# The first pass multiplies 33 of 44 up-projection weight blocks unsplit in fp32; the second pass splits and writes them

## The chip, the cores and the metric

The kernel runs on one core of a Trainium2 chip. The metric is the device time of one execution in microseconds (us), and lower is better. A change of about 0.3% (some 10 us here) is the least that a measurement of this kernel can tell from no change.

## The reference, cut to what matters

One layer of a hybrid decoder is computed for 2048 prompt tokens and 64 sample tokens, which share every weight. The part that the change touches is the gated feed-forward block:

```
x = x + W_down( SiLU(gate) * val ),  [gate|val] = causal depthwise conv (3) of RMSNorm(x) @ w_up
```

`w_up` is 1024 x 5632 in fp32, 44 blocks of 128 columns (22 for the gate, 22 for the value); `w_down` is 2816 x 1024, 22 blocks here. Around it stand the input projection, a conformer convolution with 31 taps, a gated delta-rule scan, the output projection and a per-layer embedding gate.

## The kernel before, in words

**Passes.** The tokens are worked off in six passes of 256, 384, 384, 384, 384 and 320 columns (`NTS`, the last with the sample tokens). Activations lie transposed in SBUF, channels on the partitions and tokens along the free axis, so a weight block of 1024 x 128 is eight 128 x 128 stationary tiles. The chain of stages of a pass is: input projection, scan and convolution (`units_b`), output projection (`units_w`), norm (`units_norm`), feed-forward (`units_f`), gate (`units_l`). While pass i is in its feed-forward, `merge` strews the scan and the 31-tap convolution of pass i+1 between its units; in the first pass that stretch also inverts the triangular blocks of the second pass (`inv_step`).

**Split products.** Every large product is made of three matmuls in fp32r: each operand x is held as a high part (a rounded copy, `act` at L108 on ScalarE) and a low part (the difference, `tt` at L105 on GpSimd or VectorE; both in `split`, L230). `gemm` (L280) issues for each of the eight k-tiles high x high, high x low and low x high: 24 matmuls for a block.

**Weights.** `get` (L260) keeps three blocks under way and hands out the oldest; `wblock` (L242) loads one. The pool tag "w" has three slots of 1 MB (high and low part). A block that has never been written is loaded raw (512 KB, L248) into one of three slots of the tag "xio", split into the w slot, and the pair of halves is written to DRAM (1 MB, L254). Every later pass loads the halves straight into the w slot (L245). All these DMAs are issued by one queue, SP's, in order. An exception is the set `seen`: 22 of the 44 up blocks and 11 of the 22 down blocks are split in the first pass without being written; the second pass loads them raw once more, splits them and writes them. So the first pass splits 66 blocks of the feed-forward and writes 33; the second splits and writes 33.

**Around it.** `half` (L1211) is one up block: `gemm_w` into a PSUM bank, a copy `row` and a scaled copy `y` on ScalarE, two convolution taps on VectorE (`stt`, L96). `down` (L1245) multiplies `fbuf` by a down block and adds the result to `X` on VectorE. The norm of the residual stream writes each channel block into a small tile `h` (two slots) and splits it into `q.hT2`, which `half` multiplies. The tag "X" has two slots of 128 x 8 x 384 fp32; the residual stream of each pass takes one (L1166, loaded at L1167). Instructions are issued in order on each engine; the order was set when the program was built, by priorities.

**Names in the profile.** L89 is every matmul, L93 every transpose, L96 the scalar_tensor_tensor helper, L105 the tensor_tensor helper, L108 the activation helper. `cacc` is the accumulator of the 31-tap convolution, `hT` stands for `hT2` too, `w<-raw` on POOL is the low part of a split weight block; `d`, `g` and `m` are PSUM banks.

Of the kernel before, what the change touches and what calls it, by code (L numbers as in the profile page):

```python
# [8 lines left out]
F32 = mybir.dt.float32  # L9
# [7 lines left out]
P = 128  # L17
D = 1024
KD = D // P
# [23 lines left out]
def step_kernel(  # L43
# [8 lines left out]
    V, A, G, T, SY = nc.vector, nc.scalar, nc.gpsimd, nc.tensor, nc.sync  # L52

    cpool = ctx.enter_context(tc.tile_pool(name="cpool", bufs=1))
    big = ctx.enter_context(tc.tile_pool(name="big", bufs=1))
    wp = ctx.enter_context(tc.tile_pool(name="wp", bufs=2))
# [10 lines left out]
    def nm(s):  # L67
        uid[0] += 1
        return f"{s}_{uid[0]}"
# [18 lines left out]
    def mm(out, lhsT, rhs, start, stop, skip=True):  # L88
        T.matmul(out, lhsT=lhsT, rhs=rhs, start=start, stop=stop, skip_group_check=skip)  # L89
# [8 lines left out]
    def ts(e, out, in0, s1, op0, s2=None, op1=None):  # L98
        if op1 is None:
            e.tensor_scalar(out=out, in0=in0, scalar1=s1, scalar2=None, op0=op0)  # L100
        else:
            e.tensor_scalar(out=out, in0=in0, scalar1=s1, scalar2=s2, op0=op0, op1=op1)
# [38 lines left out]
    def raw_tile(name, shape=(P, KD, P)):  # L141
        return wp.tile(list(shape), F32, tag="xio", name=nm(name), bufs=3)
# [10 lines left out]
    def h_tile(name="h"):  # L153
        return rp.tile([P, 512], F32, tag="h", name=nm(name), bufs=2)
# [75 lines left out]
    def split(src, hi, lo, hi_e="a", lo_e="g"):  # L230
        if hi_e == "a":
            act(hi, src)
        else:
            V.tensor_copy(hi, src)
        tt(G if lo_e == "g" else V, lo, src, hi.bitcast(F32), SUB)

    halves, seen = {}, set()

    def w_tile():
        return wp.tile([P, 2, KD, P], F32R, tag="w", name=nm("w"), bufs=3)  # L240

    def wblock(key, src, hi_e="a", lo_e="g", nk=KD):  # L242
        w = w_tile()
        if key in halves:
            SY.dma_start(w.bitcast(F32), halves[key])  # L245
        else:
            raw = raw_tile("raw")
            SY.dma_start(raw if nk == KD else raw.rearrange("p (k o) c -> p k (o c)", k=nk), src)  # L248
            split(raw, w[:, 0], w[:, 1], hi_e, lo_e)
            if key[0] in ("w_up", "down") and key not in seen and (key[1] // P + key[-1]) % 2:  # L250
                seen.add(key)
                return w[:, 0], w[:, 1]
            halves[key] = hw.tile([P, 2, KD, P], F32, tag=nm("halves"), name=nm("halves"))
            SY.dma_start(halves[key], w.bitcast(F32))  # L254
        return w[:, 0], w[:, 1]
# [24 lines left out]
    def gemm(ps, w, m, nk):  # L280
        whi, wlo = w
        mhi, mlo = m
        for k in range(nk):
            mm(ps, whi(k), mhi(k), k == 0, False, skip=False)
            mm(ps, whi(k), mlo(k), False, False, skip=False)
            mm(ps, wlo(k), mhi(k), False, k == nk - 1, skip=False)

    def halfs(a):
        return a[:, 0], a[:, 1]

    def gemm_w(ps, w, hT, c0, cw):
        gemm(ps, (lambda k: w[0][:, k, :], lambda k: w[1][:, k, :]),
             (lambda k: hT[0][:, k, c0:c0 + cw], lambda k: hT[1][:, k, c0:c0 + cw]), KD)
# [25 lines left out]
    def token_rs(acc, q):  # L319
        ps = bank()  # L320
        for i, (t, c0, L) in enumerate(q.tiles):
            mm(ps[:L, t:t + 1], acc[:, c0:c0 + L], one1[:, 0:1], i == 0, i == len(q.tiles) - 1)
        v = dp.tile([P, 8], F32, tag="var", name=nm("var"), bufs=2)
        rs = dp.tile([P, 8], F32, tag="rsv", name=nm("rsv"), bufs=2)
        V.memset(v, 1.0)
        ts(V, v[:, 0:q.nt], ps[:, 0:q.nt], 1.0 / D, MUL, EPS, ADD)
        if q.sam:
            ts(V, v[:NSAM, q.nt:q.nt + 1], ps[:NSAM, q.nt:q.nt + 1], 1.0 / D, MUL, EPS, ADD)
        n = len(q.tiles)
        rsqrt(rs[:, 0:n], v[:, 0:n])  # L330
        return rs
# [845 lines left out]
    def units_norm(q):  # L1177
        n = q.n

        def stats():  # L1180
            q.hT2 = big.tile([P, 2, KD, NMAX], F32R, tag="hT2", name=nm("hT2"))
            rs = token_rs(q.acc, q)
            q.dgs = []
            for t, c0, L in q.tiles:
                q.dgs.append(dp.tile([P, P], F32, tag="Zt", name=nm("dg"), bufs=ZB))
                ts(V, q.dgs[-1][:L, :L], ident[:L, :L], rs[:L, t:t + 1], MUL)

        def spread_rs():
            q.nps = ps = bank()
            for i, (t, c0, L) in enumerate(q.tiles):  # L1190
                mm(ps[:, c0:c0 + L], one1[:L, :], q.dgs[i][:L, :L], i == 0, i == len(q.tiles) - 1)

        def part(b):
            h = h_tile()
            stt(V, h[:, :n], q.X[:, b, 0:n], gains[:, b, 1:2], q.nps[:, :n], MUL, MUL)
            split(h[:, :n], q.hT2[:, 0, b, 0:n], q.hT2[:, 1, b, 0:n], "a", "v" if b % 2 else "g")
        return [((), stats), ((), spread_rs)] + [((), lambda b=b: part(b)) for b in range(KD)]


    def units_f(q):  # L1200
        n, np_, sam = q.n, q.np, q.sam
        out = []
        z = {}

        def begin():
            z["f"] = big.tile([P, 2 * FG * 2 * NMAX], F32R, tag="F", name=nm("fbuf"))
            if sam:
                z["st"] = big.tile([P, 2 * FT, 2 * NSQ], F32, tag="zs", name=nm("fst"))
                load_T("fst", [st_ffn[0].rearrange("s r c -> (s r) c")], 2 * DFF, z["st"])

        def half(col):  # L1211
            ffS = W["ff"]
            w = get()
            y = r_tile("y")
            row = r_tile("row", NMAX + 3)
            srow = srow_tile() if sam else None
            G.tensor_copy(row[:, 0:2], ffh[:, col, 0:2])  # L1217
            if sam:
                G.tensor_copy(srow[:, :, 0:2], z["st"][:, col, :].rearrange("p (s r) -> p s r", r=2))
            ps = gbank()  # L1220
            gemm_w(ps[:, :n], w, halfs(q.hT2), 0, n)
            to_row(q, row, srow, 2, ps, lambda o, i, *a: act(o, i))
            act(y[:, :n], ps[:, :n], AF.Identity, scale=ffS[:, col, 2:3], bias=ffS[:, col, 3:4])
            G.tensor_copy(ffh[:, col, 0:2], row[:, np_:np_ + 2])  # L1224
            if sam:
                G.tensor_copy(ffh[:, col, 2:18].rearrange("p (s r) -> p s r", r=2), srow[:, :, 8:10])
            for tap in (1, 0):
                for o, i in taps(q, y, row, srow, tap):
                    stt(V, o, i, ffS[:, col, tap:tap + 1], o, MUL, ADD)
            return y  # L1230

        def ff_ap(slot, hl, j, a, b):
            base = ((slot * FG + j) * 2 + hl) * NMAX
            return z["f"][:, base + a:base + b]

        def gate(f):
            z["g"] = y = half(f)
            act(y[:, :n], y[:, :n], AF.Silu)

        def val(f, slot, j):  # L1240
            y = half(FT + f)
            tt(V, y[:, :n], y[:, :n], z["g"][:, :n], MUL)
            split(y[:, :n], ff_ap(slot, 0, j, 0, n), ff_ap(slot, 1, j, 0, n))

        def down(nk, slot, i):  # L1245
            w = get()
            m = KD // nk
            for o in range(m):
                ps = bank() if q.ip == 0 and o % 2 else gbank()
                gemm(ps[:, :n], (lambda k: w[0][:, k * m + o, :], lambda k: w[1][:, k * m + o, :]),  # L1250
                     (lambda k: ff_ap(slot, 0, k, 0, n), lambda k: ff_ap(slot, 1, k, 0, n)), nk)
                xs = q.X[:, i * m + o, 0:n]
                tt(V, xs, xs, ps[:, :n], ADD)

        out.append(((), begin))
        pend = []
        for g0 in range(0, FT, FG):
            slot = (g0 // FG) % 2
            nk = min(FG, FT - g0)
            for j in range(nk):  # L1260
                f = g0 + j
                out.append(((("w_up", f * P),), lambda f=f: gate(f)))
                out.append(((("w_up", (FT + f) * P),), lambda f=f, slot=slot, j=j: val(f, slot, j)))
            out += pend
            pend = [((("down", g0, i),), lambda nk=nk, slot=slot, i=i: down(nk, slot, i)) for i in range(nk)]
        return out + pend
# [133 lines left out]
    for ip, q in enumerate(ps_):  # L1400
        prev = ps_[ip - 1] if ip else None
        nxt = None if q.sam else ps_[ip + 1]
        w = units_w(q)
        if prev is not None:
            x2 = units_x2(prev)
            w = [u for i in range(KD) for u in (w[i], x2[i])] + x2[KD:]
# [5 lines left out]
        else:  # L1412
            own = [u[1:] for u in u1 if 100 <= u[0] < 100.14 and not u[1]]
            k = len(own) // 2
# [43 lines left out]
```

## Time and profile before

| | us |
|---|---|
| median of 3 runs | 3202.05 (3193.27 to 3202.27) |
| the profiled execution, device time | 3196.92 |
| its span (first to last instruction) | 3195.2 |
| PE busy | 2973.2 |
| DVE busy | 2213.8 |
| ACT busy | 1122.4 |
| POOL busy | 894.5 |

The busy shares are means over stretches with different limits, so they are read stretch by stretch. The feed-forward of the first pass lies between 337 and 690 us of the span, that of the second between about 830 and 1340 us. "PEclk" is the granted clock of TensorE as a share of 2.4 GHz.

### The profile page before, as it was taken

The numbers are of one execution on the slowest core, as the hardware profiler recorded it, in microseconds if no ns is written. First come the engines' busy times: TensorE is split into PE (matmuls) and PEld (weight loads), VectorE is DVE, ScalarE is ACT, GpSimd is POOL, SyncE is SP. The second block draws the span as 40 slices with busy tenths as digits, with TensorE's granted clock in tenths as the row PEclk, the third lists the DMA queues.
The fourth block names the chain that finished last, engine by engine and source line by source line (L and its number), as shares of the span: only waits on it lengthen the run. The fifth ranks groups of instructions, "written<-read, shape, count | busy, mean of one in ns | idle before, by whom it ended". The sixth has DMA issues, their size and how long they took to land.

```text
span 3195.2 us, 51070 instructions
## 1 busy us (share of the span) xinstructions
PE 2973.2 (93%) x18682; PEld 2900.9 (91%) x18682; DVE 2213.8 (69%) x5378; ACT 1122.4 (35%) x2473; POOL 894.5 (28%) x1518
## 2 busy tenths in 40 slices
PE   5979688777999999999999999999999999998998
PEld 5979678677999998999999999999999999998998
DVE  6986889957669686756757666857577866743443
ACT  4333344334323334422234342223442232323223
POOL 3422576634333432211121121121131121111221
PEclk8989898888999999999999999999999999998999
DMA  7636766667777867667665677665767765666885
GB/s 231 203 118 225 239 194 214 185 214 250 297 251 248 271 231 259 237 240 249 228 220 214 237 253 245 228 239 198 249 242 255 261 241 198 219 222 226 301 293 207
DMA packets 291968, 745.28 MB, mean 233 GB/s; under 512 B 51241, under 2 KB 202282, under 8 KB 216575
## 3 DMA queue, kind: packets, MB, share of 16 engines
q1 hardware_dynamic: 291719, 742.03, 67.9%
q8 instruction: 148, 2.42, 0.3%
q14 instruction: 101, 0.83, 0.1%
HBM read 607.75 MB, written 134.57 MB: 232 GB/s over the span
## 4 chain that ended last, share of the span: by engine, by line
PE 64%; DVE 7%; DMA 3%; ACT 1%; issue 1%; SPq 0%; ACTq 0%; DVEq 0%
PE g L89 57%; PE d L89 3%; PE m L89 2%; DMA w<-halves 2%; DVE h L96 1%; PE d L93 1%; PE m L93 1%; DVE y L96 1%; DVE rt L105 1%; DVE hT L105 0%; DMA out_dram<-yt 0%; DVE cacc L96 0%; DVE sy L96 0%; DVE X L100 0%; DVE X L105 0%
## 5 line engine op out<-in xcount | busy, mean ns | idle before, releaser
L89 PE MATMUL g<-hT,w 128*128 128x384 f32 (+2 forms) x9840 | 1684.6, 329 | 38.7 <-ACT hT L108 9.3
L89 PEld LDWEIGHTS g<-hT,w 128*128 128x128 f32 x9840 | 1600.7, 192 | 49.9 <-ACT hT L108 11.0
L89 PE MATMUL g<-fbuf,w 128*128 128x384 f32 (+2 forms) x2904 | 549.4, 338 | 32.8 <-DVE X L105 15.2
L96 DVE SCALAR_TENSOR_TENSOR y<-row,ffS,y 128x384 f32<-128x384 f32 (+1 forms) x528 | 337.6, 639 | 301.8 <-ACT y L108 275.8
L89 PEld LDWEIGHTS g<-fbuf,w 128*128 128x128 f32 x2904 | 489.7, 194 | 43.3 <-DVE X L105 16.8
L96 DVE SCALAR_TENSOR_TENSOR cacc<-H,cfS,cacc 128x384 f32<-128x384 f32 (+1 forms) x696 | 487.4, 700 | 9.3 <-ACT cacc L108 3.0
L105 DVE TENSOR_TENSOR X<-X,g 128x384 f32<-128x384 f32 (+2 forms) x532 | 276.7, 524 | 228.1 <-PE g L89 225.9
L108 ACT ACTIVATE row<-g 128x384 f32<-128x384 f32 (+1 forms) x336 | 152.4, 454 | 598.5 <-PE g L89 594.2
L105 POOL TENSOR_TENSOR w<-raw,w 128x1024 fp32r<-128x1024 f32 x123 | 307.6, 2502 | 193.4 <-ACT w L108 169.9
L1224 POOL COPY ffh<-row 128x2 f32<-128x2 f32 x264 | 61.9, 235 | 594.4 <-ACT row L108 589.5
L89 PE MATMUL g<-x,w 128*128 128x384 f32 (+2 forms) x1152 | 204.1, 331 | 5.9 <-ACT w L108 4.6
L89 PE MATMUL g<-mx,w 128*128 128x384 f32 (+2 forms) x1152 | 193.9, 327 | 12.3 <-DMA w<-halves 9.5
L89 PEld LDWEIGHTS g<-mx,w 128*128 128x128 f32 x1152 | 186.7, 191 | 15.1 <-issue 4.7
L1217 POOL COPY row<-ffh 128x2 f32<-128x2 f32 x264 | 82.8, 314 | 418.2 <-DVE y L96 312.8
L89 PEld LDWEIGHTS g<-x,w 128*128 128x128 f32 x1152 | 192.1, 195 | 6.7 <-ACT w L108 5.0
L108 ACT ACTIVATE y<-g,ffS 128x384 f32<-128x384 f32 (+2 forms) x264 | 169.3, 641 | 0.1
L108 ACT ACTIVATE w<-raw 128x1024 fp32r<-128x1024 f32 x139 | 146.5, 1055 | 63.3 <-PE g L89 14.9
L105 POOL TENSOR_TENSOR fbuf<-y,fbuf 128x384 fp32r<-128x384 f32 (+2 forms) x132 | 136.4, 1034 | 115.0 <-ACT fbuf L108 111.5
L108 ACT ACTIVATE y<-y 128x384 f32<-128x384 f32 (+2 forms) x132 | 65.7, 498 | 217.7 <-DVE y L96 217.4
L108 ACT ACTIVATE fbuf<-y 128x384 fp32r<-128x384 f32 (+2 forms) x132 | 65.8, 498 | 213.5 <-DVE y L105 213.3
L96 DVE SCALAR_TENSOR_TENSOR H<-row,dnS,H 128x384 f32<-128x384 f32 (+1 forms) x144 | 92.8, 646 | 34.2 <-ACT H L108 33.2
L105 POOL TENSOR_TENSOR y<-row,y 128x256 fp32r<-128x256 f32 x48 | 36.2, 754 | 272.7 <-PE m L89 218.1
(338 smaller groups left out, 3291.1 us busy)
## 6 DMA issues: line engine op xcount, KB each, us to landing
w<-halves SPq DMA_DIRECT2D x477, 1024.0 KB
halves<-w SPq DMA_DIRECT2D x106, 1024.0 KB
raw<-in_w_up_dram SPq DMA_DIRECT2D x66, 512.0 KB
raw<-in_w_down_dram SPq DMA_DIRECT2D x33, 512.0 KB
raw<-in_w_in_dram SPq DMA_DIRECT2D x24, 512.0 KB
xt<-in_x_prompt_dram SPq DMA_DIRECT2D x16, 512.0 KB
xT<-xt SPq DMA_DIRECT2D x16, 512.0 KB
out_dram<-yt SPq DMA_DIRECT2D x16, 512.0 KB
```

Source lines behind the costliest of these rows:

```text
L89: T.matmul(out, lhsT=lhsT, rhs=rhs, start=start, stop=stop, skip_group_check=skip)
L93: T.transpose(out, in_, ident[:k, :k])
L96: return e.scalar_tensor_tensor(out=out, in0=in0, scalar=scalar, in1=in1, op0=op0, op1=op1)
L105: e.tensor_tensor(out=out, in0=a, in1=b, op=op)
L108: A.activation(out, in_, f, **kw)
L1217: G.tensor_copy(row[:, 0:2], ffh[:, col, 0:2])
L1224: G.tensor_copy(ffh[:, col, 0:2], row[:, np_:np_ + 2])
```

## The change

For an up block whose column number is not a multiple of 4 (33 of 44), the first pass loads the raw block straight into a w slot as fp32 and returns it as it is; nothing is split or written. `up_gemm` multiplies such a block by the unsplit normed activations with eight fp32 matmuls in place of 24 in fp32r. For that the first pass keeps the normed activations in fp32 (`q.hf`), in a slot of the tag "X" rather than in the small tile `h`. In the second pass these 33 blocks are loaded raw, split and written. The old exception is gone: the 11 other up blocks and all 22 down blocks are split and written in the first pass. The first pass therefore splits 33 blocks and writes 33; the second splits and writes 33, as before, but all of them up blocks.

```diff
     def wblock(key, src, hi_e="a", lo_e="g", nk=KD):
+        if key[0] == "w_up" and key[1] // P % 4 and key not in seen:
+            seen.add(key)
+            w = wp.tile([P, KD, P], F32, tag="w", name=nm("w"), bufs=3)
+            SY.dma_start(w, src)
+            return w
         w = w_tile()
...
             split(raw, w[:, 0], w[:, 1], hi_e, lo_e)
-            if key[0] in ("w_up", "down") and key not in seen and (key[1] // P + key[-1]) % 2:
-                seen.add(key)
-                return w[:, 0], w[:, 1]
             halves[key] = hw.tile([P, 2, KD, P], F32, tag=nm("halves"), name=nm("halves"))
             SY.dma_start(halves[key], w.bitcast(F32))
...
         def part(b):
-            h = h_tile()
+            if q.ip == 0:
+                if b == 0:
+                    q.hf = big.tile([P, KD, n], F32, tag="X", name=nm("hf"), bufs=2)
+                h = q.hf[:, b]
+            else:
+                h = h_tile()
...
+        def up_gemm(ps, w):
+            if isinstance(w, tuple):
+                return gemm_w(ps, w, halfs(q.hT2), 0, n)
+            for k in range(KD):
+                mm(ps, w[:, k, :], q.hf[:, k, :], k == 0, k == KD - 1, skip=False)
...
             ps = gbank()
-            gemm_w(ps[:, :n], w, halfs(q.hT2), 0, n)
+            up_gemm(ps[:, :n], w)
```

## Rows read from the trace of the kernel before

**Rows 1.** The page: busy time in all, and tenths in 40 slices of 80 us.
```profile
PE 2973.2 (93%) x18682; PEld 2900.9 (91%) x18682; DVE 2213.8 (69%) x5378; ACT 1122.4 (35%) x2473; POOL 894.5 (28%) x1518
...
DVE  6986889957669686756757666857577866743443
...
POOL 3422576634333432211121121121131121111221
```
**Rows 2.** Windows: stretch, length, busy us of each engine, clock, DMA.
```profile
core 0: us, PE busy (x) PEld busy (x) DVE busy (x) ACT busy (x) POOL busy (x), PEclk, DMA share, GB/s
337.00:650.00 313.00, 247.30 (x1748) 234.81 (x1748) 297.31 (x508) 132.54 (x277) 205.91 (x203) 0.88 0.67 203
450.00:600.00 150.00, 120.64 (x904) 116.88 (x905) 145.99 (x231) 65.62 (x141) 104.53 (x98) 0.90 0.69 211
900.00:1300.00 400.00, 384.47 (x2296) 376.98 (x2296) 287.72 (x618) 143.18 (x301) 126.23 (x174) 0.99 0.73 250
```
**Rows 3.** Waits of PE, 450 to 600: us in total, times, longest us.
```profile
PE d L89 <- DVE nw L96: 10.3, 2, 5.8
PE d L89 <- DVE vn L105: 6.6, 2, 5.4
PE d L89 <- DVE ke L105: 4.8, 1, 4.8
PE g L89 <- DVE X L105: 4.4, 2, 3.3
```
**Rows 4.** Timeline of DVE, then of POOL, around 483: start us, us, instruction.
```profile
482.45 0.60 DVE L96 SCALAR_TENSOR_TENSOR cacc<-H,cfS,cacc 128x384 f32<-128x384 f32 x1
...
483.31 2.43 DVE L96 SCALAR_TENSOR_TENSOR cacc<-H,cfS,cacc 128x384 f32<-128x384 f32 x1
...
490.56 1.00 DVE L96 SCALAR_TENSOR_TENSOR y<-row,ffS,y 128x256 f32<-128x256 f32 x2
...
482.66 2.66 POOL L105 TENSOR_TENSOR w<-raw,w 128x1024 fp32r<-128x1024 f32 x1 [1.06 <-ACT w L108]
```
**Rows 5.** Groups: two of DVE, 450 to 600; the first's like, 1400 to 1700.
```profile
L96 DVE SCALAR_TENSOR_TENSOR cacc<-H,cfS,cacc 128x384 f32<-128x384 f32 x73 | 76.3, 1045 | 0.7
L96 DVE SCALAR_TENSOR_TENSOR y<-row,ffS,y 128x256 f32<-128x256 f32 x40 | 35.0, 875 | 2.4 <-ACT y L108 2.1
...
L96 DVE SCALAR_TENSOR_TENSOR cacc<-H,cfS,cacc 128x384 f32<-128x384 f32 x99 | 62.3, 629 | 1.7 <-ACT cacc L108 0.8
```
**Rows 6.** Groups: low parts of split weights on POOL, 337 to 650, and 450 to 600.
```profile
L105 POOL TENSOR_TENSOR w<-raw,w 128x1024 fp32r<-128x1024 f32 x58 | 146.4, 2527 | 30.9 <-ACT w L108 30.5
...
L105 POOL TENSOR_TENSOR w<-raw,w 128x1024 fp32r<-128x1024 f32 x30 | 75.9, 2532 | 14.0 <-ACT w L108 13.8
```
**Rows 7.** PE: two fp32r rows of the timeline, one fp32, the fp32 form's durations.
```profile
518.96 5.62 PE L89 MATMUL g<-hT,w 128*128 128x256 f32 x46
681.60 0.28 PE L89 MATMUL m<-fbuf,w 128*128 128x256 f32 x1
...
304.88 1.02 PE L89 MATMUL d<-kd,Lm 128*128 128x256 f32 x4
...
L89 PE MATMUL d<-kd,Lm x64: 377/379/767, 80.2 to 2391.1; 128*128 128x256 f32 x64
```
**Rows 8.** Waits of SP's queue, then of PE, 337 to 650.
```profile
SPq L254 <- POOL w L105: 129.4, 25, 11.4
SPq L248 <- POOL w L105: 66.4, 21, 6.1
...
PE g L89 <- POOL w L105: 10.8, 10, 2.9
```
**Rows 9.** Chain of waits: a raw block's landing; SP's timeline: loads of the residual stream.
```profile
797.97 4.28 DMA raw<-in_w_up_dram
...
294.10 4.38 SPq L1167 DMA_DIRECT2D X<-xT  x2
```
**Rows 10.** Waits of SP's queue in the second pass, 850 to 1250.
```profile
SPq L254 <- POOL w L105: 110.5, 16, 9.7
```

## The prediction

> **What bounds the kernel now.** I read the page's busy table first, then its 40 slices, then the windows and waits of the stretch that the change touches. By the whole span PE is the bound with 93% [rows 1]. The slices show that this isn't so everywhere: in the fifth to eighth slice (320 to 640 us) DVE reaches its highest digits and POOL its own [rows 1]. The windows tell the two regimes apart. In 337 to 650, the first pass's feed-forward but for its end, DVE is busy 297.3 of 313 us (95%), PE 247.3 (79%) and the granted clock is 0.88; in 900 to 1300, the second pass's, PE is busy 384.5 of 400 us (96%) at a clock of 0.99 [rows 2]. In the first of these PE waits mostly for DVE: the four longest waits of 450 to 600 make 26.1 of the 29.4 us that PE stands idle there [rows 2, 3].
>
> Why is DVE full? The same step of the 31-tap convolution, 128x384, takes 0.60 us, and 2.43 us when it starts while POOL is at the low part of a weight block [rows 4]. The groups say it in bulk: 1045 ns a step in 450 to 600, where POOL splits 30 blocks, and 629 ns in 1400 to 1700, where it splits none [rows 5, 6]. So a split on POOL takes time from DVE, and DVE is what PE waits for.
>
> **The splits that go.** In the first pass 66 feed-forward blocks are split; 33 will be. In plan order each six blocks (four up, two down) lose three splits, so of the 58 in 337 to 650 [rows 6] 29 go. What one takes from DVE: from below, (1.045 - 0.629) x 73 + (0.875 - 0.50) x 40 = 45 us over the 30 splits of 450 to 600, 1.5 us each, for two forms alone [rows 4 to 6]; from above, 2.43 - 0.60 = 1.83 us, a step fully held up [rows 4]. I take 1.6, near the lower end, which is a mean, with something for the forms left out. DVE gives back 29 x 1.6 = 46 us (44 to 53) and would stand at 251 us. POOL's own 29 x 2.5 us and ScalarE's copies bound nothing here (206 and 133 of 313 us [rows 2]); at most they end PE's 10.8 us of waits for a split block [rows 8]. I count none of that.
>
> **The matmuls that come.** A fp32r matmul of 256 columns follows the one before by (5.62 - 0.28) / 45 = 0.119 us, so a block of 24 takes 2.85 us [rows 7]. An fp32 matmul of 256 columns appears as two instructions; four of them take 1.02 us, (1.02 - 0.379) / 3 = 0.214 us apart, so eight matmuls are 16 x 0.214 = 3.42 us [rows 7]. Each block costs PE 0.57 us more at the full clock. About 31 of the 33 lie in 337 to 650: 18 us, or 20 us at that stretch's clock of 0.88. At half the clock throughout it would be twice, 35 us; that is the upper end, and 18 the lower. PE then needs 247 + 20 = 267 us.
>
> Row and rule differ here. The Trainium skill, FP8 and Floating Point Precision, TensorE Precision Notes, counts true fp32 as four passes through the array; with one pass for each of the three fp32r products a block would grow by a third, 0.95 us instead of 0.57 as an estimate, and the gain below would be some 12 us smaller (3184 us). [...]
>
> **What is late next.** DVE at 251 and PE at 267 us change places, narrowly. PE reaches 96% where it alone is the bound [rows 2], but here the order was fixed at build time and DVE will still be near 90%, so PE will go on meeting some waits. With 96% the stretch takes 278 us, with 90% 297; I take 93%, 287 us, a gain of 26. The best case is that PE's half-rate spells go with its waits (267 x 0.88 / 0.95 = 247 us): then DVE sets the end at its present 95%, 264 us, a gain of 49. The rest of the stage, to 690 us, loses four more splits: 2 us.
>
> **What is moved.** DMA: the first pass still has 66 raw loads and 33 writes (11 up and 22 down in place of 22 and 11), the second still 33 raw loads, 33 splits and 33 writes. Bytes are the same; squeezed into 287 us, 203 GB/s become 221, under the 250 of 900 to 1300 [rows 2]. In the second pass SP's queue waits for POOL before its writes, 110.5 us in 400, and the loads of later blocks stand behind [rows 10]; PE is still 96% busy, so that is hidden by the three blocks under way. The raw blocks there now come three in a row instead of mixed; I take 1 us lost. In the first pass 58 raw blocks cost PE 10.8 us of such waits [rows 8], so 33 may cost up to 6.
>
> The norm writes the same eight tiles elsewhere: nothing. But `hf` holds the second "X" slot, in which the second pass's residual stream was loaded at 294 us, long ahead [rows 9]. Now this load of 1.5 MB waits on SP for the last unsplit up block, and behind it in the queue stand the weights of the last down blocks and of the output projection, on which PE waits. At 203 GB/s [rows 2] it takes 7.7 us; the four down blocks still to be multiplied (4 x 2.85 us) cover it. I take 2 us, bounds 0 and 8.
>
> An unsplit block's load also has a new wait: it needs the w slot itself, where a raw block needed only an "xio" slot. It may start when PE is done with the block three before, two blocks (2 x 287/58 = 9.9 us) ahead of its use, and a raw block lands in 4.28 us [rows 9]. That leaves 5.6 us for SP to be late; its waits for POOL average (129.4 + 66.4) / 46 = 4.3 us [rows 8]. I take nothing.
>
> **Sum.** -26 - 2 + 1 + 2 = -25 us against the profiled execution's 3196.9: 3172 us. The median of the runs is 5 us above that execution, their lowest 4 below, so I leave 3172 as it is.
>
> **Rivals.**
> PE stays below its best: it fills only 88% because DVE (251 of 303 us) still keeps it in the same places. The stretch takes 303 us and the kernel 3188 us. For it: two engines close to full, in a fixed order.
> DVE sets the end, as above: 3197 - 49 + 1 = 3149 us. For it: the low clock is in a stretch with waits; against it: fp32 adds to PE in every group.
> Slower, first: PE's idle 65.7 us [rows 2] are the scan's own back and forth between PE and DVE, not a full DVE. Then they stay, and PE's added 20 us land on the end: 3217 us. It decides if fewer than 20 us of idle time go. Against it: the longest waits, 5 us and more [rows 3], are far longer than the small steps waited for, and DVE is never free meanwhile. The Trainium skill, Perfetto Trace Analysis, Identifying the Most-Contended Engine, would have the busiest engine relieved first, which over the whole span is PE; the same page says that regimes differ along a kernel, and the windows show that this one does.
> Slower, second: SP's queue is late for unsplit loads. Its longest wait, 11.4 us [rows 8], is 5.8 us over the room; one such load in each of 11 groups of six blocks costs 64 us, 3236 us. It decides from 25 / 33 = 0.8 us a load. Against it: the mean wait fits, and half the waits for POOL go.
>
> **How the numbers follow.** Forecast 0.63 (3158 to 3186), PE below its best 0.13, DVE the bound 0.10, slower by idle time that stays 0.07, by late loads 0.07. About 0.3% is the least a measurement of this kernel can tell: below 3192.4 is faster. The forecast, the DVE case and a third of the 88% case lie there, 0.77; the rest of that case and a little of the slower ones lie within, 0.11; slower 0.12. The range runs from the DVE case to the near edge of the 88% case with all small terms against it (8 + 6 us, less what was counted): 3148 to 3198.
>
> **What would show it.** In the stage's window the convolution step falls from 1045 ns towards 840; POOL's split count halves; a block of unsplit matmuls takes 3.4 us; PE's share rises above 90% and DVE's falls to about 88%; its end moves from 690 to about 663 us; from there to the end nothing changes by more than a few us. I am wrong if PE's waits for DVE stay at 26 us in 150, if waits for DMAs into w take their place, or if the clock falls with fp32.

## The result

The changed kernel takes 3145.48 us (median of 4 runs, 3140.98 to 3149.25) against 3202.16 before (3193.27 to 3206.09). The ratio is 0.9833, with a 95% interval of 0.9811 to 0.9855. The direction was forecast; the size was not: 57 us by the medians where the likeliest case said 25 to 30, and the median lies 2.5 us below the low end of the range. By its time the case that came was "DVE sets the end" (3149 us), which had a chance of 0.10; by its mechanism it came in part, as the section on the prediction says.

To see where the time went, cut both spans at four points of PE's timeline: the first matmul of the first pass's first up block, the last one of its last up block, and the first ones of the second and of the third pass's output projection.

| stretch | before | after | difference |
|---|---|---|---|
| up to the first up block ("lead") | 337.3 | 330.9 | -6.4 |
| first to last up block ("up stretch") | 330.0 | 278.0 | -52.0 |
| from there to the second pass's output projection ("tail") | 20.8 | 31.5 | +10.7 |
| the second pass, to the third's output projection | 556.2 | 561.2 | +5.0 |
| all later passes | 1950.9 | 1945.9 | -5.0 |
| span | 3195.2 | 3147.5 | -47.7 |

The later passes are the same work in both. Over all the runs below they take 1940 to 1953 us, so 5 us there mean nothing.

The windows of the changed kernel over the up stretch, its steady part, the tail and the second pass; columns as in [rows 2] (length; busy PE, PEld, DVE, ACT, POOL; clock; DMA share; GB/s):

```profile
330.90:608.90 278.00, 249.72 (x1527) 227.87 (x1528) 241.70 (x505) 104.28 (x246) 124.48 (x174) 0.94 0.73 224
450.00:580.00 130.00, 118.36 (x761) 108.30 (x761) 117.16 (x218) 49.47 (x123) 61.60 (x81) 0.96 0.75 230
608.90:640.40 31.50, 17.10 (x109) 15.81 (x107) 21.72 (x50) 19.21 (x36) 18.52 (x14) 0.81 0.88 323
640.40:1201.60 561.20, 520.98 (x3100) 509.35 (x3101) 398.53 (x854) 208.48 (x421) 197.83 (x252) 0.96 0.75 255
```

The kernel before, cut at the same points (up stretch and tail):

```profile
337.30:667.30 330.00, 256.28 (x1802) 243.33 (x1803) 307.64 (x526) 142.70 (x293) 213.90 (x208) 0.87 0.65 197
667.30:688.10 20.80, 14.42 (x90) 13.44 (x90) 15.87 (x28) 9.78 (x21) 14.29 (x13) 0.84 0.72 223
```

DVE's busy time in the up stretch falls by 66 us and PE's doesn't grow: 249.7 us after 256.3, with fp32 in it. PE's share rises from 78 to 90%, DVE's falls from 93 to 87%, and the granted clock, a mean over spells at 2.4 and at 1.2 GHz, rises from 0.87 to 0.94: by that mean 0.26 x 330 = 86 us of the stretch were at 1.2 GHz before and 0.12 x 278 = 33 us are now.

PE's waits in the steady part of the changed kernel (who waited for whom: us in total, times, longest), and DVE's groups there, which answer to [rows 3] and [rows 5]; then POOL's low parts, and one fp32 block in PE's timeline:

```profile
PE g L89 <- DMA w<-in_w_up_dram: 5.8, 2, 4.2
PE g L89 <- DVE y L96: 2.2, 2, 1.1
PE g L89 <- DVE X L105: 2.0, 1, 2.0
...
L96 DVE SCALAR_TENSOR_TENSOR cacc<-H,cfS,cacc 128x384 f32<-128x384 f32 x72 | 53.0, 735 | 1.0
L96 DVE SCALAR_TENSOR_TENSOR y<-row,ffS,y 128x256 f32<-128x256 f32 x38 | 27.1, 714 | 7.0 <-ACT y L108 6.5
...
L105 POOL TENSOR_TENSOR w<-raw,w 128x1024 fp32r<-128x1024 f32 x15 | 38.6, 2576 | 13.0 <-ACT w L108 10.9 <-DMA w<-in_w_up_dram 1.2 <-POOL T L815 0.6
...
484.17 3.67 PE L89 MATMUL g<-hf,w 128*128 128x256 f32 x16
```

The long waits of the scan's matmuls for DVE (`nw`, `vn`, `ke`) are gone; the largest that is left is a new wait for the unsplit blocks' loads. The convolution step falls from 1045 to 735 ns. An fp32 block's 16 instructions are (3.67 - 0.38) / 15 = 0.219 us apart, 3.5 us a block.

### The profile page after: what moved, and what is told of

Same layout as the page of the kernel before. It is cut to its first block, busy times and chain, and to the rows that moved or that the text cites. A ratio compares the mean times of both kernels' runs of the same rounds, so it can differ in the third digit from the quotient of the medians.

```text
span 3147.5 us, 50438 instructions
## 1 busy us (share of the span) xinstructions
PE 2966.5 (94%) x18418; PEld 2886.3 (92%) x18418; DVE 2144.5 (68%) x5378; ACT 1093.1 (35%) x2440; POOL 810.3 (26%) x1485
## 4 chain that ended last, share of the span: by engine, by line
PE 63%; DVE 8%; DMA 5%; ACT 1%; issue 1%; SPq 0%; POOL 0%; DVEq 0%; ACTq 0%; POOLq 0%
PE g L89 56%; PE d L89 3%; DMA w<-halves 3%; PE m L89 2%; DVE h L96 1%; PE d L93 1%; DVE y L96 1%; PE m L93 1%; DVE cacc L96 1%; DVE X L100 0%; DVE hT L105 0%; DVE rt L105 0%; DVE H L96 0%; DVE tv L105 0%; DVE zs L105 0%
## 5 line engine op out<-in xcount | busy, mean ns | idle before, releaser
L89 PE MATMUL g<-hT,w 128*128 128x384 f32 (+2 forms) x9048 | 1580.3, 332 | 35.6 <-DMA w<-halves 11.9
L89 PEld LDWEIGHTS g<-hT,w 128*128 128x128 f32 x9048 | 1499.4, 191 | 44.9 <-ACT hT L108 10.8
L89 PE MATMUL g<-fbuf,w 128*128 128x384 f32 (+2 forms) x2904 | 534.9, 334 | 21.8 <-ACT w L108 8.4
L96 DVE SCALAR_TENSOR_TENSOR y<-row,ffS,y 128x384 f32<-128x384 f32 (+1 forms) x528 | 321.5, 609 | 296.5 <-ACT y L108 271.3
L89 PEld LDWEIGHTS g<-fbuf,w 128*128 128x128 f32 x2904 | 477.9, 189 | 31.5 <-DVE X L105 11.2
L96 DVE SCALAR_TENSOR_TENSOR cacc<-H,cfS,cacc 128x384 f32<-128x384 f32 (+1 forms) x696 | 452.8, 651 | 10.6 <-ACT cacc L108 3.7
L105 POOL TENSOR_TENSOR w<-raw,w 128x1024 fp32r<-128x1024 f32 x90 | 223.9, 2488 | 183.9 <-ACT w L108 169.8
L89 PE MATMUL g<-hf,w 128*128 128x256 f32 x528 | 128.0, 398 | 10.9 <-DMA w<-in_w_up_dram 7.1
L108 ACT ACTIVATE w<-raw 128x1024 fp32r<-128x1024 f32 x106 | 112.0, 1056 | 55.0 <-PE g L89 24.2
L89 PEld LDWEIGHTS g<-hf,w 128*128 128x128 f32 x528 | 103.7, 202 | 26.1 <-issue 4.4
```

The costliest lines, as they stand in the source:

```text
L96: return e.scalar_tensor_tensor(out=out, in0=in0, scalar=scalar, in1=in1, op0=op0, op1=op1)
L105: e.tensor_tensor(out=out, in0=a, in1=b, op=op)
L108: A.activation(out, in_, f, **kw)
```

## The experiments

All are cut at the same points. The stretches come from each kernel's profiled execution; the whole is that execution's time (the only run of e1 to e8), and the median of four runs for e9 to e11. The kernel before, run beside them, took 3199.9 us (e1 to e4), 3193.6 us (e5 to e8) and 3189.98 to 3205.36 us (seven runs, e9 to e11).

| kernel | lead | up stretch | tail | second pass | whole, us |
|---|---|---|---|---|---|
| before | 337.3 | 330.0 | 20.8 | 556.2 | 3196.9 |
| after | 330.9 | 278.0 | 31.5 | 561.2 | 3149.3 |
| e1, `hf` alone | 335.4 | 332.3 | 18.2 | 553.0 | 3189.3 |
| e2, splits kept, fp32 | 333.3 | 328.9 | 27.1 | 560.5 | 3203.2 |
| e3, no low part, no fp32 | 334.2 | 268.1 | 23.4 | 557.2 | 3127.8 |
| e4, before, 33 low parts on DVE | 337.4 | 300.9 | 20.8 | 552.3 | 3166.1 |
| e5, 22 unsplit | 336.1 | 297.5 | 25.9 | 551.6 | 3153.1 |
| e6, 44 unsplit | 331.9 | 259.4 | 30.3 | 574.8 | 3144.1 |
| e7, `hf` in another buffer | 336.9 | 272.0 | 30.9 | 560.4 | 3143.0 |
| e8, first pass's splits on DVE | 332.2 | 254.4 | 30.5 | 564.1 | 3123.8 |
| e9, second pass's too | 333.2 | 252.2 | 29.3 | 552.3 | 3111.2 |
| e10, 22 unsplit, first pass on DVE | 332.3 | 273.1 | 24.5 | 545.2 | 3118.5 |
| e11, 22 unsplit, both on DVE | 333.6 | 272.5 | 24.8 | 541.7 | 3117.7 |

**e2: fp32 without sparing the splits.**

```diff
-            w = wp.tile([P, KD, P], F32, tag="w", name=nm("w"), bufs=3)
-            SY.dma_start(w, src)
-            return w
+            w = w_tile()
+            raw = raw_tile("raw")
+            SY.dma_start(raw, src)
+            split(raw, w[:, 0], w[:, 1], hi_e, lo_e)
+            return w[:, 0].bitcast(F32)
```

> The changed kernel, but the 33 blocks are loaded raw and split in the first pass as well (copy on ScalarE, low part on GpSimd, not written), and the fp32 matmuls take the high part, so the low part is left out of these products. Theory A (the splits on GpSimd take time from VectorE, 1.6 us each): VectorE stays full, the first up block to the last takes the 330 us of before or more, the convolution step's mean stays above 1000 ns, and the whole is 3190 to 3215 us. Rival B (the gain came from fp32 in place of three products, or from a calmer clock with it): the up stretch stays near 278 us and the whole near 3150.

The window of its up stretch, and the convolution step in it:

```profile
333.30:662.20 328.90, 270.79 (x1538) 243.54 (x1539) 304.27 (x523) 136.92 (x283) 210.04 (x208) 0.88 0.62 189
...
L96 DVE SCALAR_TENSOR_TENSOR cacc<-H,cfS,cacc 128x384 f32<-128x384 f32 x116 | 118.1, 1018 | 2.5 <-ACT cacc L108 1.2
```

The up stretch stays at 329 us. Theory A held, and three things follow. The gain isn't fp32's. The clock isn't fp32's either: with PE's waits left in place it is 0.88, as before. And fp32's price on PE is there, 270.8 us busy against 256.3, while the stretch gets no longer: as long as DVE is full, PE's extra 14.5 us lie in its idle time. So the rival in which PE's idle time stays and the added work lands on the end is refuted too.

**e3: the low part left out, no fp32.**

```diff
-            w = wp.tile([P, KD, P], F32, tag="w", name=nm("w"), bufs=3)
-            SY.dma_start(w, src)
-            return w
+            w = w_tile()
+            raw = raw_tile("raw")
+            SY.dma_start(raw, src)
+            act(w[:, 0], raw)
+            return w[:, 0], w[:, 0]
```

> The changed kernel, but the 33 blocks keep ScalarE's rounded copy and 24 fp32r matmuls; only the low part on GpSimd is left out, and the copy stands in for it, so these products are wrong by the low part. Theory A: VectorE gets its 52 us back as in the changed kernel, and PE saves the 0.57 us a block that fp32 costs; if PE is what ends the up stretch of the changed kernel it gets 10 to 20 us shorter than 278; if VectorE ends it, it stays at 272 to 280. Rival B (the way of the weights sets the pace: raw slot, copy, split): the stretch goes back towards 300 us or more, since ScalarE's copies and the detour through a raw slot are back.

```profile
334.20:602.30 268.10, 232.77 (x1799) 224.83 (x1800) 242.46 (x521) 136.99 (x282) 134.78 (x176) 0.93 0.76 240
...
PE g L89 <- DVE X L105: 16.3, 6, 6.7
```

That window is its up stretch, with PE's longest wait in it. The kernel leaves the low part out: the rounded copy stands in its place in the 24 matmuls, so PE's work stays, with the high part twice and the low part nowhere. Without the 33 low parts on GpSimd DVE comes to 242.5 us, the changed kernel's 241.7, though the raw slot and ScalarE's copies are back: the way of the weights isn't what paid. PE is 17 us less busy than in the changed kernel and the stretch 10 us shorter. So fp32 does seem to cost something once DVE is relieved, but no more than about 10 of its 19 us (33 x 0.57). It may be less: e3 also lacks the waits for unsplit blocks' loads (7.1 us in the changed kernel's up stretch), and e7 below, with the changed kernel's splits and matmuls, comes to 272.0 us. PE still waits for DVE in e3, so neither engine alone sets the end.

**e4: the kernel before, the low parts moved to DVE.**

```diff
-            split(raw, w[:, 0], w[:, 1], hi_e, lo_e)
+            split(raw, w[:, 0], w[:, 1], hi_e, "v" if key[0] == "w_up" and key[1] // P % 4 and key not in seen else lo_e)
```

> The kernel before, but for the same 33 up blocks the low part is made by VectorE in the first pass instead of GpSimd (1.22 us each by the kernel before). Theory A: each costs VectorE 1.22 us of its own and spares it the 1.6 us that it lost beside GpSimd: the up stretch is 5 to 20 us shorter than 330, and no VectorE step is stretched except beside the other splits; whole 3180 to 3197 us. Rival B (VectorE isn't what bounds, or it doesn't lose time to GpSimd): 33 x 1.22 = 40 us more on VectorE and the whole is 3215 to 3245 us.

Its up stretch, and in it the convolution step and the low parts that DVE now makes itself:

```profile
337.40:638.30 300.90, 244.22 (x1802) 233.24 (x1803) 287.72 (x558) 141.84 (x286) 155.65 (x177) 0.90 0.71 216
...
L96 DVE SCALAR_TENSOR_TENSOR cacc<-H,cfS,cacc 128x384 f32<-128x384 f32 x116 | 95.2, 821 | 0.5
L105 DVE TENSOR_TENSOR w<-raw,w 128x1024 fp32r<-128x1024 f32 x32 | 40.7, 1273 | 2.4 <-ACT w L108 2.3
```

DVE gets 40.7 us of work more and is 20 us less busy. The direction is theory A's; the 29 us by which the stretch is shorter are above its 5 to 20. DVE's other instructions take 307.6 - (287.7 - 40.7) = 60.6 us less for the 32 low parts moved, so a low part on GpSimd cost DVE 1.9 us, against 1.27 for making it itself. DVE's lower busy time makes 20 of the 29 us. What the other 9 are (a block is also ready sooner, 1.27 us instead of 2.5, and the clock is 0.90 instead of 0.87) wasn't tried apart.

**e5 and e6: how many blocks.**

```diff
-        if key[0] == "w_up" and key[1] // P % 4 and key not in seen:
+        if key[0] == "w_up" and key[1] // P % 2 and key not in seen:
```

and, for e6,

```diff
-        if key[0] == "w_up" and key[1] // P % 4 and key not in seen:
+        if key[0] == "w_up" and key not in seen:
```

> The changed kernel with 22 blocks unsplit (every odd column) instead of 33. Theory A (the gain goes with the number of splits that no longer run on GpSimd, VectorE still full): up stretch between before and after in proportion, 330 - 22/33 x 52 = 295 us, 290 to 300, whole about 3160. Rival B (PE already sets the end at 33, so that the last 11 gave little): the stretch is 278 to 285 us, whole 3143 to 3152.

> The changed kernel with all 44 up blocks unsplit in the first pass; 44 are then split and written in the second. Theory A (VectorE sets the end at 33): 11 x 1.6 = 18 us less on VectorE, up stretch 260 to 268 us. Rival B (PE and VectorE are level at 33): PE gets 6 us more, the stretch stays at 274 to 284 us. For the second pass both expect no more than 6 us more, since PE bounds it: whole 3135 to 3155 us.

The windows of the up stretch and of the second pass, first e5, then e6:

```profile
336.10:633.60 297.50, 251.83 (x1620) 231.18 (x1620) 263.26 (x522) 116.51 (x261) 148.91 (x185) 0.92 0.77 248
659.50:1211.00 551.50, 518.36 (x3101) 507.10 (x3100) 388.67 (x860) 199.61 (x414) 171.47 (x244) 0.97 0.73 252
```

```profile
331.90:591.30 259.40, 246.22 (x1440) 221.98 (x1440) 228.12 (x500) 94.78 (x238) 98.10 (x164) 0.98 0.65 198
621.60:1196.40 574.80, 527.77 (x3099) 515.27 (x3100) 417.55 (x858) 218.63 (x435) 226.42 (x266) 0.95 0.78 262
```

The up stretch is 330.0, 297.5, 278.0 and 259.4 us with 0, 22, 33 and 44 blocks unsplit: 1.5, 1.8 and 1.7 us a block, 1.6 over all. No knee shows, though with e7's 272.0 us for 33 blocks the last two steps would be 2.3 and 1.1. The stretches are theory A's in both runs (e6's 259.4 just under its 260 to 268); e5's whole, 3153 us, lies between rival B's 3143 to 3152 and A's 3160. This doesn't show that VectorE alone sets the end: with 44 blocks PE is busy 95% of the stretch and DVE 88%. PE has room for the fp32 because its clock is 0.98 there; its busy time is lower than at 22 despite 22 fp32 blocks more. The second pass takes the opposite course, 551.6, 561.2 and 574.8 us with 22, 33 and 44 blocks to split: about 1.1 us for each block passed on to it. e6's 13.6 us there were forecast as at most 6.

**e1 and e7: the load of the residual stream.** e1 is the kernel before with `hf` in the second "X" slot and one small read of it at the last up block; e7 is the changed kernel with `hf` in the buffer that the mixer output has left.

```diff
-            h = h_tile()
+            if q.ip == 0:
+                if b == 0:
+                    q.hf = big.tile([P, KD, n], F32, tag="X", name=nm("hf"), bufs=2)
+                h = q.hf[:, b]
+            else:
+                h = h_tile()
...
+            if q.ip == 0 and col == 2 * FT - 1:
+                act(t_tile('hx')[:, :n], q.hf[:, 0])
```

> The kernel before with one part of the change alone: the first pass writes its normed activations to the second slot of the tag X and holds it to the last up block (one small read there keeps it); all splits and matmuls are as before. Theory A: the load of the second pass's residual stream, put off by this, explains the 6.5 us that the stretch ahead of the first up block lost and the 11 us that the stretch from the last up block to the next output projection gained in the changed kernel. Then the first falls from 337.3 to about 331 us, the second rises from 21 to about 30 us, and the up stretch between stays near 330 us: about 3195 to 3205 us in all. Rival B: both shifts come from the weight blocks' new order (fewer raw blocks early, down blocks split late). Then both stretches stay as before, 337 and 21 us.

```diff
-                    q.hf = big.tile([P, KD, n], F32, tag="X", name=nm("hf"), bufs=2)
+                    z7["t"] = big.tile([P, KD * n + B * B + B * 16], F32, tag="H1", name=nm("hf"))
+                    q.hf = z7["t"][:, 0:KD * n].rearrange("p (k n) -> p k n", n=n)
...
-            zf = big.tile([P, B * B + B * 16], F32, tag="H1", name=nm("zf")) if second else z.zf
+            zf = z7["t"][:, KD * NTS[0] * P:] if second else z.zf
```

> The changed kernel with the first pass's unsplit activations in another buffer (the one that the first pass's mixer output has just left, shared with the scratch of the block inversion), so that the second pass's residual stream is loaded at about 295 us again. Theory A: in the changed kernel this load stood at 609 us in SP's queue, waiting for the last unsplit up block, with the raw loads of the last down blocks behind it; without it PE's wait of 8 us for the first of them goes and the stretch from the last up block to the output projection falls from 31.6 to 20 to 24 us, while the stretch ahead grows by 0 to 6 us: 3136 to 3147 us. Rival B: the last down blocks are late for another reason (their splits follow one another on ScalarE and GpSimd): the stretch stays at 30 us or more.

SP's timeline around the tail in the changed kernel, and PE's wait in it; then one row of SP's in the kernel before, whose last up block ends at 667.3 us:

```profile
601.39 5.63 SPq L1308 DMA_DIRECT2D row<-in_w_ple_dram  x2
608.87 0.34 SPq L1169 DMA_DIRECT2D X<-xT  x1
609.26 0.94 SPq L253 DMA_DIRECT2D raw<-in_w_down_dram  x2
...
617.84 0.58 PE L89 MATMUL g<-fbuf,w 128*128 128x256 f32 x1 [8.13 <-ACT w L108]
...
654.77 6.67 SPq L248 DMA_DIRECT2D raw<-in_w_down_dram  x3
```

The same queue in e7, where the residual stream is loaded at 296 us, and PE's waits in its tail:

```profile
601.38 5.63 SPq L1310 DMA_DIRECT2D row<-in_w_ple_dram  x2
607.11 0.93 SPq L254 DMA_DIRECT2D raw<-in_w_down_dram  x2
...
PE g L89 <- DVE X L105: 6.3, 2, 3.6
PE g L89 <- ACT w L108: 5.1, 3, 3.5
```

Theory A falls for the tail. In e1 the load is just as late (671 us, after the last up block) and the tail is short, 18.2 us; in e7 it is early and the tail stays at 30.9, as rival B had it. In the changed kernel and e7 the last four raw down blocks are issued from 609 and 607 us on, when PE has all but finished the up blocks, and behind two loads for the gate stage that SP was held up with; the kernel before issues three of its last four at 655 to 661 us, ahead of the end of its up blocks. So SP's queue, which has another order in the changed program, comes late to the last down blocks. That this makes the tail longer fits these rows but wasn't tried, nor whether the order of the writes or the two gate loads is behind it. The lead is 331 to 336 us in every kernel in which the load doesn't stand there, against 337 in the three where it does (before, e4, e7): putting the load off gives 1 to 6 us there. The whole gains nothing by it: e7's lead is 6.0 us longer than the changed kernel's, its up stretch 6.0 us shorter. e1's whole, 3189 us, lies below its 3195 to 3205.

**e8 to e11: the remaining splits on DVE.** If a low part on GpSimd costs DVE more than DVE's own 1.2 us, the other 33 should move. e8 moves those of the first pass's feed-forward; e9 those of the second pass as well; e10 is e8 and e11 is e9 with 22 blocks unsplit.

```diff
-            split(raw, w[:, 0], w[:, 1], hi_e, lo_e)
+            split(raw, w[:, 0], w[:, 1], hi_e, "v" if key[0] in ("w_up", "down") and key not in seen else lo_e)
```

> The changed kernel with the 33 splits that the first pass's feed-forward still makes (11 up, 22 down) taken from GpSimd to VectorE: 1.22 us each of VectorE's own in place of what it loses beside GpSimd. Theory A (what a split on GpSimd costs VectorE is over 1.6 us, as the run with 33 blocks' low part on VectorE gave 29 us): VectorE gets shorter by 10 to 30 us, the up stretch falls to 255 to 272 us, until PE ends it. Rival B (PE ends the up stretch already): it stays at 274 to 284 us.

> The changed kernel with all feed-forward splits of the first and of the second pass on VectorE. In the runs so far the second pass took 552 us with 22 up blocks to split, 561 with 33 and 575 with 44. Theory A (there too the price is paid beside GpSimd, through VectorE): it falls from 564 (first-pass splits on VectorE alone) to 550 to 556 us, the whole to 3108 to 3118 us. Rival B (the price is in the path of the weights: raw load, split and write in one queue): the second pass stays at 560 to 566 us, the whole near 3124 us.

> The changed kernel with 22 blocks unsplit instead of 33 and the first pass's other feed-forward splits on VectorE. Theory A (with VectorE at 1.22 us a split PE ends the up stretch at 254 us, and 11 fewer fp32 blocks give PE 6 us): the up stretch is 250 to 262 us, the second pass 550 to 556 us, the whole 3108 to 3120 us. Rival B (VectorE still ends it): the up stretch is 268 us or more (11 x 1.22 us more), the whole 3122 to 3130 us.

> The same with the second pass's splits on VectorE too. If the price there is paid beside GpSimd, the second pass falls below 550 us and the whole to 3098 to 3112 us; if it is the path of the weights, both stay where the run with 22 unsplit blocks has them, within 4 us.

Windows of the up stretch and the second pass: e8, then e9, then e10 (with PE's longest wait in its up stretch), then e11 (the second pass alone).

```profile
332.20:586.60 254.40, 242.20 (x1530) 222.23 (x1531) 225.56 (x538) 107.08 (x250) 73.26 (x147) 0.96 0.79 244
617.10:1181.10 564.00, 525.71 (x3099) 515.24 (x3100) 396.83 (x854) 208.40 (x421) 197.32 (x252) 0.95 0.74 254
```

```profile
333.20:585.30 252.10, 237.49 (x1530) 217.69 (x1531) 225.30 (x538) 106.81 (x250) 73.55 (x147) 0.99 0.80 247
614.70:1167.00 552.30, 519.32 (x3106) 508.83 (x3107) 388.37 (x892) 211.71 (x427) 121.08 (x219) 0.97 0.76 260
```

```profile
332.30:605.30 273.00, 244.19 (x1620) 224.48 (x1620) 234.07 (x558) 118.41 (x262) 65.53 (x147) 0.94 0.86 272
629.80:1175.00 545.20, 516.07 (x3100) 504.65 (x3101) 386.34 (x854) 196.54 (x410) 168.92 (x241) 0.98 0.73 253
...
PE g L89 <- DMA w<-in_w_up_dram: 12.0, 9, 3.3
```

```profile
630.90:1172.60 541.70, 516.61 (x3099) 505.98 (x3100) 373.06 (x876) 198.41 (x410) 116.88 (x219) 0.97 0.73 255
```

e8 shortens the up stretch by another 24 us, to the lower edge of its theory A; PE is now busy 95% of it. DVE's other instructions take 241.7 - (225.6 - 34.5) = 50.6 us less for the 28 low parts moved in that window, 1.8 us each.

e9 takes 12 us from e8's second pass, into the 550 to 556 us of its theory A. But e11, which does the same to e10 with 22 blocks to split, takes only 3.5 us (545.2 to 541.7) and under 1 us of the whole: both stay within the 4 us of its other case, and its 3117.7 us miss the 3098 to 3112. The kernels with the same 33 splits on GpSimd there differ among themselves by 7 us (after, e2, e3, e7 and e8: 557 to 564). So it isn't shown that the price in the second pass is paid beside GpSimd. Most of it seems to lie elsewhere: with all those low parts on VectorE, 11 blocks more to split still cost 10.6 us (e11 to e9), about 1 us each as in e5 to e6. PE's longest wait there is for the loads of written halves in both, 15.9 us (e9) and 9.6 us (e11); what delays them wasn't tried.

e9 has the lowest median: 3111.18 us (4 runs, 3106.94 to 3112.25), 0.9724 of before (0.9703 to 0.9745), but the intervals of e10 and e11 overlap with its own. e10 (0.9746, 0.9724 to 0.9769) and e11 (0.9747, 0.9718 to 0.9776) show the exchange: against e8, e10 gives back 19 us in the up stretch for 11 blocks and gains 19 in the second pass and 6 in the tail; against e9, e11 gives back 20 and gains 11 and 5. e10 missed its 250 to 262 us: PE is only 89% busy there, DVE 86%, and the DMA share is the highest of these up stretches, 0.86. The 273 us are in the range of its rival B, whose cause, a full VectorE, the 86% don't bear out: PE's longest wait is for the loads of unsplit blocks, 12.0 us in nine waits. What delays those loads wasn't tried, so its limit stays open.

## Why the prediction was right in sign and short in size

**What bounds.** Right. DVE was full in the first pass's feed-forward because of POOL's low parts (e2, e3, e4, e8).

**The splits that go.** Right in mechanism, too small in size. I took 1.6 us of DVE's time for a split, with 1.83 as the upper bound. DVE's busy time falls by 66 us for 33 splits in the changed kernel, 2.0 us each; e3 against e2 gives 61.8 us for 32, e4 60.6 for 32 and e8 50.6 for 28, 1.8 to 1.9 us each. The convolution step fell to 735 ns where I had forecast 840. That the line of e5, the changed kernel and e6 gives 1.6 us a block as well is luck: this is what the stretch gets shorter, after fp32's work on PE and the new waits. The count of 29 was taken for the stretch to 650 us; with the four near its end all 33 paid.

**The matmuls that come.** The price of a block was right (3.42 us forecast, 3.5 measured); in e2, 33 of them added 14.5 us to PE's busy time where 19 were expected. As to the four passes of the Trainium skill (FP8 and Floating Point Precision, TensorE Precision Notes), the ratio to a fp32r block's 2.85 us [rows 7] is about 1.2 here, as the rows before had it, not the 4/3 estimated from them. Why isn't settled. It isn't that the fp32r matmuls of 256 columns are too short: in the trace of the kernel before they start 0.117 us apart and those of 384 columns 0.175, as much for each column.

**What is late next.** This step failed, in its largest term, PE's busy time. I added 20 us to PE's 247 at the clock of before and called the case in which the half-rate spells go with PE's waits "the best case". That case is what happened: 256.3 us of PE work, plus 19 for fp32 at full clock, became 249.7, most of the difference because the clock rose from 0.87 to 0.94 (275 x 0.87 / 0.94 = 255; the other 5 us stay open). e2 and e3 show the link: the same fp32 with the waits left in place keeps 0.88 and 270.8 us, and in e3, without fp32 but with PE's idle time down from 74 to 35 us, the clock is 0.93. The low clock came and went with the waits that I had just read as caused by DVE, so the two should have been priced together. The best case gave 264 us for a stretch of 313, a gain of 49; the up stretch of 330 gained 52. The 93% that I took for PE's share was, besides, a little too high (90%).

**What is moved.** The residual stream's load was put at 2 us (0 to 8). The tail did grow, by 10.7 us, beyond the upper bound, but e1 and e7 show that this load isn't why. The lead's 6.4 us weren't foreseen. The second pass was put at 1 us lost (up to 6) and lost 5, which is less than the 7 us between kernels with the same splits there; over e5, the changed kernel and e6 it does lose about 1.1 us a block, so it hides less than I read from its busy share. The wait for w slots was taken as nothing and is 7.1 us in the up stretch (three waits, the longest 4.2).

**The rivals.** "PE stays below its best" and both slower cases are out. "DVE sets the end" came nearest: PE's low clock went with its waits, as that case says, but DVE isn't at the 95% by which it was reckoned. It is at 87% and PE at 90%, and the stretch gets shorter by relieving either one (e3 takes work from PE, e8 from DVE). That the case's 3149 us lie 4 us from the median is partly luck, since the tail's 10.7 us and the second pass's 5.0 are set off by 6.4 in the lead and 5.0 in the later passes; of all these it had 1 us.

## What to carry to other kernels

When the waits of TensorE are to go, price its clock together with them: here the time lost at the low clock went with the waits, and it paid for the work that was added. A kernel whose whole span is PE's may still have a stretch that another engine holds up; there PE can have room for dearer matmuls that spare that engine work. And before an operation is parked on GpSimd "because it is free", compare VectorE's instructions beside it with the same ones alone.

## What the runs showed of the hardware

A low part on GpSimd (2.5 us) took 1.8 to 2.0 us from DVE in four pairs of kernels, more than the 1.2 us in which DVE makes it itself. What a DVE instruction loses beside it depends on where its inputs lie. Groups of the up stretch, first the changed kernel, then e8, where GpSimd makes no low part; `y<-y,y` reads two SBUF tiles, `X<-X,m` of the same size reads one of its two from PSUM:

```profile
L105 DVE TENSOR_TENSOR y<-y,y 128x256 f32<-128x256 f32 x21 | 23.8, 1136 | 0.2
...
L105 DVE TENSOR_TENSOR X<-X,m 128x256 f32<-128x256 f32 x36 | 14.7, 410 | 0.1
```

```profile
L105 DVE TENSOR_TENSOR X<-X,m 128x256 f32<-128x256 f32 x36 | 15.0, 416 | 3.5 <-PE m L89 3.3
L105 DVE TENSOR_TENSOR y<-y,y 128x256 f32<-128x256 f32 x21 | 8.9, 424 | 0.1
```

1136 against 424 ns for the one, 410 against 416 for the other. The first is a mean of two kinds. A long one in the changed kernel, and the low part that POOL makes beside it:

```profile
461.73 2.50 DVE L105 TENSOR_TENSOR y<-y,y 128x256 f32<-128x256 f32 x1
...
461.61 2.34 POOL L105 TENSOR_TENSOR w<-raw,w 128x1024 fp32r<-128x1024 f32 x1 [0.98 <-ACT w L108]
```

Of the 21 `y<-y,y` there, eight of the nine that run beside a low part take 1.95 to 2.57 us and all others 0.41 to 0.42; the seven `X<-X,m` beside one take 0.41 like the rest. The Trainium skill, SBUF — State Buffer, Who interferes with whom, has this as a rule: a DVE instruction with two SBUF inputs contends with a GpSimd instruction that reads SBUF; one with at most one SBUF input, outside the 2-port perf modes, doesn't. The trace agrees. What I hadn't expected is that each block split in the second pass lengthens it by about 1.1 us, though PE is busy 92 to 95% of it. That this is the same price isn't shown: with the low parts on VectorE it is still about 1 us (e11 to e9), and its cause stays open.
